# Two dense and three score banks of PSUM, woven attention work, and undivided differential maps in a two-layer encoder trunk

## The chip, the cores and the metric

The kernel runs on one core of a Trainium2 chip. The metric is the device time of one execution in microseconds (us). The kernel before takes 1228.05 us, the median of three runs (1227.83 to 1228.29). All engines of the core work side by side: PE multiplies matrices into the accumulators of PSUM, DVE and ACT do the elementwise work and alone read PSUM, POOL does elementwise work in SBUF, and SP issues the transfers.

## The reference

The input is 512 tokens of width 1024 in float32. There are two layers, and each has this shape:

```python
h = rmsnorm(x, attn_norm[l])
proj = einsum('bsd,de->bse', h, w_in[l])                 # 1024 -> 3072
sb_q, sb_k, sb_v, df_q, df_k, df_v = split(proj, ...)
# stick-breaking heads (8 of width 64), strictly causal:
#   w = sigmoid(z) * exp(reversed cumulative sum of log sigmoid(-z), without itself)
# differential heads (4, each with 2 maps of width 64), rope on q and k, causal by chunks of 64:
p = softmax(where(allowed, s, neg), axis=-1)
attn = p[:, :, 0] - lam * p[:, :, 1]
df_out = rmsnorm(attn @ v, subln_norm[l]) * (1 - lambda_init)
x = x + concat(sb_out, df_out) @ w_o[l]
h = rmsnorm(x, mlp_norm[l])
x = x + square(relu(h @ w_ff1[l])) @ w_ff2[l]            # 1024 -> 4096 -> 1024
```

A final rmsnorm follows. The rmsnorm over a differential head's output adds 1e-6 to the mean square before the root.

## The kernel before

Everything lies transposed: x is held as 8 tiles of 128 channels by 512 tokens. A product in float32 precision is made of three matmuls (function `three`, lines 260 to 262), with each operand split into a high and a low part: ACT rounds to the high part (L119 for weights, L207 for data) and DVE subtracts it (L120, L208). Weights come in units of 128x1024 through three raw buffers and two split buffers.

The attention of a layer is two streams woven into one. `dense()` makes the projections in blocks of 24 matmuls, one block for each 128 output channels, in the order d0 w0 d1 w1 ... s0 u0 ... s3 u3: d is the query and key of a differential pair, w its value, s the query and key of a stick-breaking pair, u its value. A block of the value is multiplied by the norm factor rbc (L400), then transposed through PSUM (L405, `vT`) and split (L412, L413). Differential queries and keys get rope from two DVE products (L463, L464) and two POOL sums (L471, L472); stick-breaking ones are scaled (L442). Their halves are moved by SP (L437), and for differential keys copied by ACT (L458), into stacked tiles. Behind the projections `dense()` makes the half of the output projection that takes the differential heads (`wo(1)`, 8 blocks of 12 matmuls, added to x at L699). The other half, `wo(0)`, comes when the attention is through.

`attn()` is the other stream. It goes through 24 units, 8 differential and 16 stick-breaking, and for unit i it makes the scores (`s1_df`, `s1_sb`), then the transposes of the weights of unit i-2 (`s2`, tiles T...), then the products with the values of unit i-3 (`s3`, tiles O...). In `s1_df` two matmuls (L499, L500) make a score tile; DVE masks it (L539 or L543) and reduces it to its negated maximum (L540 or L544), and ACT takes the exponential with the row sum (L552). Then both sums are inverted (L558), the second is multiplied by minus lambda (L559), POOL divides the first map (L560), and DVE adds the second (L561). In `s1_sb` ACT makes two sigmoids (L514, L515), DVE a product scan (L517), POOL the weight (L520).

A differential head's output is squared, and its norm factor goes through a transpose of the squares into PSUM and a reduction (`rms_a`, tile rs_d, L231 to L245), and through two matmuls that spread the factor (`rms_b`, tile rb_d, L253, L254). `start_norm` and `finish` issue the two in the next two steps of `attn()`.

The main loop takes one piece of `dense()` after the other and lets `attn()` run whenever its share of time, by costs written in the code, has come. This gives the order of the program; a scheduler of the framework then orders the instructions of each engine, and PE keeps that order. Each engine works through its queue strictly in order.

PSUM has eight banks of 128x512. They are shared out by tags: "t" has 2 (transposes T and vT, rs and rb tiles), "mm" has 3 (dense blocks, output projection, feed-forward), "s" has 2 (scores and two early projection blocks), and "o" has 1 (products with the values).

The feed-forward of a layer goes in two halves of 16 blocks (`block`, evicted at L783), each followed by 8 output blocks of 48 matmuls (L812). At the end of layer 1 the last units and the final norm are in `finale`.

Of the kernel before, what the change touches and what calls it, by code (L numbers as in the profile page):

```python
# [9 lines left out]
F32 = mybir.dt.float32  # L10
# [3 lines left out]
ALU = mybir.AluOpType  # L14
# [127 lines left out]
def trunk(ctx, tc, xT, w, gains, lamv, cos, sin, out):  # L142
# [6 lines left out]
    def bank(tag, name, bufs=2):  # L149
        return ps.tile([P, 512], F32, tag=tag, name=name, bufs=bufs)  # L150
# [76 lines left out]
    def rms_a(src, inv_n, col, name, eng, dgt):  # L227
        pt = bank("t", "rs_" + name)
        if RST and eng is not nc.gpsimd or RST == 2:
            for j in range(4):  # L230
                nc.tensor.transpose(pt[:, j * P : (j + 1) * P], src[:, j * P : (j + 1) * P], ident)  # L231
            nc.vector.tensor_reduce(out=ms, in_=pt.rearrange("p (j f) -> p j f", j=4), axis=AX.X, op=ALU.add)
            nc.vector.tensor_scalar(out=ms, in0=ms, scalar1=inv_n, scalar2=EPS, op0=ALU.mult, op1=ALU.add)
        else:
            for j in range(4):
                nc.tensor.matmul(pt[:, j : j + 1], src[:, j * P : (j + 1) * P], ones, start=True, stop=True)
            nc.vector.tensor_scalar(out=ms, in0=pt[:, 0:4], scalar1=inv_n, scalar2=EPS, op0=ALU.mult, op1=ALU.add)
        nc.gpsimd.tensor_tensor(out=col, in0=ms, in1=mhalf, op=ALU.pow)
        nc.vector.tensor_copy(chi, col)
        nc.vector.tensor_sub(clo, col, chi.bitcast(F32))  # L240
        dg_hi, dg_lo = dgt("dgh" + name), dgt("dgl" + name)
        idb = ident.unsqueeze(1).to_broadcast([P, 4, P])
        eng.tensor_mul(
            dg_hi.rearrange("p (j t) -> p j t", j=4), idb, chi.bitcast(F32).unsqueeze(2).to_broadcast([P, 4, P]))
        eng.tensor_mul(  # L245
            dg_lo.rearrange("p (j t) -> p j t", j=4), idb, clo.unsqueeze(2).to_broadcast([P, 4, P]))

        return dg_hi, dg_lo

    def rms_b(bc, name, dg):  # L250
        dg_hi, dg_lo = dg
        pb = bank("t", "rb_" + name)
        nc.tensor.matmul(pb, ones_r.to_broadcast([P, P]), dg_hi, start=True, stop=False)  # L253
        nc.tensor.matmul(pb, ones_r.to_broadcast([P, P]), dg_lo, start=False, stop=True)  # L254
        nc.scalar.copy(bc, pb)
# [14 lines left out]
    def block(name, tag="mm"):  # L270
        pt = bank(tag, name, 3 if tag == "mm" else 2)
# [23 lines left out]
    def finale(us, pool, small):  # L295
# [13 lines left out]
        def stage2(t, r):  # L309
            tk = slice(256 * t, 256 * t + 256)  # L310
            pb = bank("o", f"rb_f{t}", 1)
# [14 lines left out]
        tags = (("mm", 3), ("s", 2), ("mm", 3), ("s", 2), ("mm", 3))  # L326
        pts, sqs = [], []
        for t in range(2):
            tk = slice(256 * t, 256 * t + 256)
            for db in range(KC):  # L330
                tag, n = tags[(t * KC + db) % 5]
                sqf = pool.tile([P, 256], F32, tag="sqf", name=f"sqf{t}{db}", bufs=3)
                pt = bank(tag, f"fe{t}{db}", n)[:, 0:256]
# [17 lines left out]
    for l in range(L):  # L351
        with ExitStack() as actx:
# [45 lines left out]
            def evict_v(pt, kind, b, which):  # L398
# [3 lines left out]
                def rest():  # L402
                    tv = bank("t", f"vT{l}{kind}{b}")
# [16 lines left out]
            heads = {}  # L420

# [102 lines left out]
            def s1_df(u):  # L524
                b, half = u["b"], u["half"]
                st = {w: stacks[("d", b, w)] for w in "qk"}
                u["w"] = []
                for i in (2 * half, 2 * half + 1):
                    wd = P * (i + 1)
                    nm = f"{l}d{b}{i}"  # L530
                    sm = a3.tile([P, 6], F32, tag="sm", name="sm" + nm, bufs=4)
                    pr = []
                    both = bank("s", f"S{nm}") if wd <= 256 else None
                    for m in range(2):
# [13 lines left out]
                        if both is None or m == 1:  # L548
                            for mm, (pp, ss) in enumerate(pr):
                                if both is None and mm < m:  # L550
# [3 lines left out]
                                    accum_out=sm[:, 2 + mm : 3 + mm])  # L554
# [3 lines left out]
                    nc.vector.reciprocal(sm[:, 4:6], sm[:, 2:4])  # L558
                    nc.vector.tensor_mul(sm[:, 5:6], sm[:, 5:6], nlam[:, l : l + 1])  # L559
                    nc.gpsimd.tensor_mul(pr[0][:, 0:wd], pr[0][:, 0:wd], sm[:, 4:5].to_broadcast([P, wd]))  # L560
                    nc.vector.scalar_tensor_tensor(  # L561
                        out=pr[0][:, 0:wd], in0=pr[1][:, 0:wd], scalar=sm[:, 5:6], in1=pr[0][:, 0:wd],
# [34 lines left out]
            def s3(u):  # L597
                half, b, m, kind = u["half"], u["b"], u["m"], u["kind"]
                key = (kind, b, m)
                if half == 0:  # L600
                    heads[key] = bank("o", f"O{l}{kind}{b}{m}", 1)
# [61 lines left out]

            def attn():
                n = len(units)
                stage = 0
                for i in range(n + LAG3):
                    stage = stage + 1 if late else 0
                    if i < n:
# [3 lines left out]
                        yield from (s1_sb if u["kind"] == "s" else s1_df)(u)  # L673
                    if stage == 1:
                        yield start_norm()
                    if 0 <= i - LAG2 < n:
                        yield from s2(units[i - LAG2])
                    if stage == 2:
                        yield finish()
                        stage = 0  # L680
                    if 0 <= i - LAG3 < n:
                        while not ok(("v" + units[i - LAG3]["kind"], units[i - LAG3]["b"])):
                            yield 0
                        yield from s3(units[i - LAG3])
# [20 lines left out]
            def dense():  # L705
                step, held = 0, []
                if l == 0:
                    b = int(ORDER[0][1])
                    us = [W.next("x"), W.next("x")]
                    pts = [bank("mm", f"p0{i}", 3) for i in range(2)]  # L710
# [51 lines left out]
        with ExitStack() as fctx:  # L762
# [25 lines left out]
            for half in range(2):  # L788
                us = []
                for f in range(HC):  # L790
                    step = 0
                    for pt in block(f"f{l}_{half}_{f}"):
# [12 lines left out]
                for db in range(KC):  # L805
                    pt = bank("mm", f"f2_{l}{half}{db}", 3)
# [74 lines left out]
```

## Time and profile before

| what | us |
|---|---|
| median of three runs | 1228.05 |
| the profiled execution, its own time | 1228.06 |
| its span, first to last instruction | 1226.3 |
| attention of layer 0, about 0 to 262 | 262 |
| feed-forward of layer 0, about 262 to 611 | 349 |
| attention of layer 1, about 611 to 862 | 251 |
| feed-forward of layer 1 and finale, about 862 to 1226 | 364 |

The profile is of one execution. A row of a timeline has the start, the duration (of several instructions where they are merged), the engine, the line, the operation, the tile written and the tiles read, and in brackets how long the engine had been idle and what ended that. A row of waits has the waiting instruction, the one waited for, the sum, the number of times and the longest. PEld is PE's loading of weights, which runs beside the matmuls. PEclk is the share of full clock that PE was granted. Names in rows leave out buffer numbers: S0d is a differential score of layer 0, p0d its exponential map, T0d its transpose, O0d the product with the values; with s in place of d they are the stick-breaking ones. In the text a score's name goes on with the pair of heads, the row block and, for the two wide row blocks, the map: S0d121 is layer 0, pair 1, row block 2, map 1.

### The profile page before, as it was taken

What the parts mean: (1) busy time and instruction counts of PE and PEld (TensorE: products, weight loads), DVE (VectorE), ACT (ScalarE), POOL (GpSimd) and SP (SyncE); (2) the same over time, 40 slices, a digit from 0 to 9 for tenths busy, and PEclk for the clock granted to TensorE, in tenths of its full rate; (3) what the DMA queues carried; (4) which work ended last, traced back from release to release, by engine and by line L of the source; (5) the groups of instructions that cost most, each with busy time, mean ns of one, the idle gap of its engine ahead of it and who ended that gap; (6) DMA issues with size and microseconds to landing.
All of it is one profiled execution on the core that took longest, in us unless ns stands there. A gap on an engine that the chain in (4) does not pass through costs nothing.

```text
span 1226.3 us, 15312 instructions
## 1 busy us (share of the span) xinstructions
PE 1194.8 (97%) x5658; PEld 991.6 (81%) x5658; DVE 680.1 (55%) x1016; ACT 551.6 (45%) x932; POOL 202.3 (16%) x260
## 2 busy tenths in 40 slices
PE   9989999999999999999998999999999999999996
PEld 6777878888888888888887788888888888888886
DVE  7778877764532334433367887886544322544325
ACT  5666665553431234423347765665443221443114
POOL 1313543230000000001122344432100000000002
PEclk9999999999999999999999999999999999999998
DMA  7344443222233232232234344432223233232221
GB/s 250 78 137 133 119 136 104 68 87 104 87 102 101 88 103 95 94 104 90 100 97 132 110 128 118 123 103 70 94 96 103 89 101 103 86 103 91 90 95 69
DMA packets 46890, 128.16 MB, mean 105 GB/s; under 512 B 7264, under 2 KB 10336, under 8 KB 46816
## 3 DMA queue, kind: packets, MB, share of 16 engines
q1 hardware_dynamic: 46672, 127.17, 33.0%
q8 instruction: 45, 0.74, 0.2%
q14 instruction: 29, 0.24, 0.1%
q10 hardware_dynamic: 144, 0.02, 0.0%
HBM read 104.09 MB, written 2.10 MB: 87 GB/s over the span
## 4 chain that ended last, share of the span: by engine, by line
PE 85%; DVE 4%; ACT 3%; POOL 2%; issue 1%; SPq 1%; DMA 0%; DVEq 0%; POOLq 0%; ACTq 0%
PE f L260 19%; PE f L262 19%; PE f L261 19%; PE wo L261 2%; PE wo L260 2%; PE wo L262 2%; DVE wlo L120 1%; SPq L437 1%; PE T1s L580 1%; PE T0s L580 1%; PE O1s L609 0%; PE O0s L609 0%; PE O1s L608 0%; PE O0s L608 0%; PE S1d L499 0%
## 5 line engine op out<-in xcount | busy, mean ns | idle before, releaser
L119 ACT ACTIVATE whi<-raw 128x1024 fp32r<-128x1024 f32 (+2 forms) x198 | 203.2, 1028 | 480.0 <-PE f L261 427.2
L120 DVE TENSOR_TENSOR wlo<-raw,whi 128x1024 fp32r<-128x1024 f32 (+2 forms) x198 | 242.0, 1224 | 147.1 <-ACT whi L119 146.2
L260 PE MATMUL f<-h_hi,whi 128*128 128x512 f32 x512 | 199.4, 389 | 0.0
L262 PE MATMUL f<-h_hi,wlo 128*128 128x512 f32 x512 | 199.2, 389 | 0.0
L261 PE MATMUL f<-h_lo,whi 128*128 128x512 f32 x512 | 199.2, 389 | 0.0
L260 PE MATMUL f<-uh,whi 128*128 128x512 f32 x496 | 192.9, 389 | 0.0
L261 PE MATMUL f<-ul,whi 128*128 128x512 f32 x496 | 192.9, 389 | 0.0
L262 PE MATMUL f<-uh,wlo 128*128 128x512 f32 x496 | 192.9, 389 | 0.0
L783 DVE SCALAR_TENSOR_TENSOR ft<-f,rbc 128x512 f32<-128x512 f32 x64 | 44.3, 692 | 163.8 <-PE f L262 162.8
L262 PEld LDWEIGHTS f<-h_hi,wlo 128*128 128x128 f32 x512 | 96.1, 188 | 20.1
L261 PEld LDWEIGHTS f<-h_lo,whi 128*128 128x128 f32 x512 | 96.1, 188 | 20.0
L260 PEld LDWEIGHTS f<-h_hi,whi 128*128 128x128 f32 x512 | 96.1, 188 | 19.8
L261 PEld LDWEIGHTS f<-ul,whi 128*128 128x128 f32 x496 | 93.1, 188 | 19.4
L262 PEld LDWEIGHTS f<-uh,wlo 128*128 128x128 f32 x496 | 93.1, 188 | 19.4
L260 PEld LDWEIGHTS f<-uh,whi 128*128 128x128 f32 x496 | 93.1, 188 | 19.2
L221 POOL TENSOR_TENSOR ssq<-ssq,sq 128x512 f32<-128x512 f32 x21 | 34.8, 1656 | 374.3 <-ACT sq L220 365.2
L812 DVE TENSOR_TENSOR x<-x,f 128x512 f32<-128x512 f32 x32 | 22.0, 688 | 103.0 <-PE f L262 103.0
L342 POOL TENSOR_TENSOR ssq<-ssq,sqf 128x256 f32<-128x256 f32 x6 | 4.4, 737 | 338.4 <-ACT sqf L340 335.0
L208 DVE TENSOR_TENSOR ul<-fu,uh 128x512 fp32r<-128x512 f32 x64 | 44.1, 692 | 0.4 <-ACT uh L207 0.4
L207 ACT ACTIVATE uh<-fu 128x512 fp32r<-128x512 f32 x64 | 40.6, 635 | 2.0
L784 ACT ACTIVATE fu<-ft 128x512 f32<-128x512 f32 x64 | 39.7, 620 | 1.6 <-DVE ft L783 1.6
L520 POOL TENSOR_TENSOR sig1s<-sig1s,C1s 128x128 f32<-128x128 f32 (+3 forms) x32 | 30.0, 939 | 55.3 <-DVE C1s L517 40.9
(725 smaller groups left out, 2173.5 us busy)
## 6 DMA issues: line engine op xcount, KB each, us to landing
raw<-in_w SPq DMA_DIRECT2D x176, 512.0 KB, 3.5
raw<-in_w SPq DMA_DIRECT2D x16, 448.0 KB, 3.1
x<-in_xT SPq DMA_DIRECT2D x8, 256.0 KB, 4.4
out_xT<-y SPq DMA_DIRECT2D x8, 256.0 KB, 2.4
raw<-in_w SPq DMA_DIRECT2D x8, 128.0 KB, 4.3
cos_t<-in_cos SPq DMA_DIRECT2D x2, 256.0 KB, 3.8
sin_t<-in_sin SPq DMA_DIRECT2D x2, 256.0 KB, 3.6
kl0d0k<-l0d0k SPq DMA_DIRECT2D x8, 64.0 KB, 2.0
```

Source lines behind the costliest of these rows:

```text
L119: h = nc.scalar.activation(hi[:, a:b], raw[:, a:b], AF.Copy)
L120: self.last = h, nc.vector.tensor_tensor(out=lo[:, a:b], in0=raw[:, a:b], in1=hi[:, a:b].bitcast(F32), op=ALU.subtract)
L207: nc.scalar.activation(hi, src, AF.Copy)
L208: nc.vector.tensor_tensor(out=lo, in0=src, in1=hi.bitcast(F32), op=ALU.subtract)
L221: return s, eng.tensor_tensor(out=ssq, in0=ssq, in1=sq, op=ALU.add)
L260: nc.tensor.matmul(pt, ah, bh, start=first, stop=False)
L261: nc.tensor.matmul(pt, ah, bl, start=False, stop=False)
L262: nc.tensor.matmul(pt, al, bh, start=False, stop=last)
L520: nc.gpsimd.tensor_mul(sig[:, 0:wd], sig[:, 0:wd], C[:, 1 : wd + 1])
L580: nc.tensor.transpose(pt[:, off : off + P], u["w"][qi][:, kb * P : (kb + 1) * P], ident)
L783: nc.vector.scalar_tensor_tensor(out=t, in0=pt, scalar=0.0, in1=rbc, op0=ALU.max, op1=ALU.mult)
L784: nc.scalar.activation(uu, t, AF.Square)
```

## The change

It has four parts.

1. PSUM: "mm" gets 2 banks, "s" 3. A new tag "any" takes the five of both in the turn mm, s, s, mm, s; it is used by the feed-forward, the finale and `wo(0)`. `vT` of the stick-breaking values and `rb_d` go from "t" to "s". In layer 0 the projection block at step 16 goes to "s" too, and in layer 1 that at 16 instead of that at 32.
2. `attn()`: the rest of a step (start of the norm, transposes of unit i-2, end of the norm, values of unit i-3) is a generator of its own, and one piece of it is issued behind every piece of the scores, where before it came behind all scores of the unit.
3. The maps are not divided: the first map stays as the exponential gave it, and the second is added with the factor minus lambda times the first sum over the second. POOL's division L560 is gone.
4. The head's output is so larger by the first row sum, which its rmsnorm takes out again. Only the 1e-6 has to grow by the square of that sum: `start_norm` makes a small tile `floor` from the kept sums (`tops`), and `rms_a` adds it.

```diff
-    def bank(tag, name, bufs=2):
-        return ps.tile([P, 512], F32, tag=tag, name=name, bufs=bufs)
+    banks = {"t": 2, "mm": 2, "s": 3, "o": 1}
+    turn = [0]
+
+    def bank(tag, name):
+        if tag == "any":
+            tag = ("mm", "s", "s", "mm", "s")[turn[0] % 5]
+            turn[0] += 1
+        return ps.tile([P, 512], F32, tag=tag, name=name, bufs=banks[tag])
...
-    def rms_a(src, inv_n, col, name, eng, dgt):
+    def rms_a(src, inv_n, col, name, eng, dgt, floor=None):
...
-            nc.vector.tensor_scalar(out=ms, in0=ms, scalar1=inv_n, scalar2=EPS, op0=ALU.mult, op1=ALU.add)
+            if floor is None:
+                nc.vector.tensor_scalar(out=ms, in0=ms, scalar1=inv_n, scalar2=EPS, op0=ALU.mult, op1=ALU.add)
+            else:
+                nc.vector.scalar_tensor_tensor(
+                    out=ms, in0=ms, scalar=inv_n, in1=floor, op0=ALU.mult, op1=ALU.add)
...
-    def rms_b(bc, name, dg):
+    def rms_b(bc, name, dg, tag="t"):
         dg_hi, dg_lo = dg
-        pb = bank("t", "rb_" + name)
+        pb = bank(tag, "rb_" + name)
...
-        tags = (("mm", 3), ("s", 2), ("mm", 3), ("s", 2), ("mm", 3))
...
-                pt = bank(tag, f"fe{t}{db}", n)[:, 0:256]
+                pt = bank("any", f"fe{t}{db}")[:, 0:256]
...
-                    tv = bank("t", f"vT{l}{kind}{b}")
+                    tv = bank("s" if kind == "u" else "t", f"vT{l}{kind}{b}")
...
+                if half == 0:
+                    tops[b] = a3.tile([P, 4], F32, tag="top", name=f"top{l}{b}", bufs=3)
+                top = tops[b]
...
-                    sm = a3.tile([P, 6], F32, tag="sm", name="sm" + nm, bufs=4)
+                    sm = a3.tile([P, 5], F32, tag="sm", name="sm" + nm, bufs=4)
+                    sums = (top[:, i : i + 1], sm[:, 2:3])
...
-                    nc.vector.reciprocal(sm[:, 4:6], sm[:, 2:4])
-                    nc.vector.tensor_mul(sm[:, 5:6], sm[:, 5:6], nlam[:, l : l + 1])
-                    nc.gpsimd.tensor_mul(pr[0][:, 0:wd], pr[0][:, 0:wd], sm[:, 4:5].to_broadcast([P, wd]))
+                    nc.vector.reciprocal(sm[:, 3:4], sums[1])
                     nc.vector.scalar_tensor_tensor(
-                        out=pr[0][:, 0:wd], in0=pr[1][:, 0:wd], scalar=sm[:, 5:6], in1=pr[0][:, 0:wd],
+                        out=sm[:, 4:5], in0=sums[0], scalar=nlam[:, l : l + 1], in1=sm[:, 3:4],
+                        op0=ALU.mult, op1=ALU.mult)
+                    nc.vector.scalar_tensor_tensor(
+                        out=pr[0][:, 0:wd], in0=pr[1][:, 0:wd], scalar=sm[:, 4:5], in1=pr[0][:, 0:wd],
                         op0=ALU.mult, op1=ALU.add)
...
             def start_norm():
                 b, os_, sqo, rc = late[0]
-                dgs[b] = rms_a(sqo, 1.0 / P, rc, f"d{l}{b}", nc.gpsimd, tr)
+                floor = a3.tile([P, 4], F32, tag="floor", name=f"floor{l}{b}")
+                nc.vector.scalar_tensor_tensor(
+                    out=floor, in0=tops[b], scalar=EPS, in1=tops[b], op0=ALU.mult, op1=ALU.mult)
+                dgs[b] = rms_a(sqo, 1.0 / P, rc, f"d{l}{b}", nc.gpsimd, tr, floor)
...
-                rms_b(rb, f"d{l}{b}", dgs[b])
+                rms_b(rb, f"d{l}{b}", dgs[b], "s")
...
+            def behind_scores(i, stage):
+                n = len(units)
+                if stage == 1:
+                    yield start_norm()
+                if 0 <= i - LAG2 < n:
+                    yield from s2(units[i - LAG2])
+                if stage == 2:
+                    yield finish()
+                if 0 <= i - LAG3 < n:
+                    while not ok(("v" + units[i - LAG3]["kind"], units[i - LAG3]["b"])):
+                        yield 0
+                    yield from s3(units[i - LAG3])
 
             def attn():
...
+                    rest = behind_scores(i, stage)
...
-                        yield from (s1_sb if u["kind"] == "s" else s1_df)(u)
...
+                        front = (s1_sb if u["kind"] == "s" else s1_df)(u)
+                        for cost in front:
+                            yield cost
+                            nxt = 0
+                            while nxt == 0:
+                                nxt = next(rest, None)
+                                if nxt is not None:
+                                    yield nxt
+                    yield from rest
...
-                        pt = bank("mm", f"wo{l}{half}{db}", 3)
+                        pt = bank("mm" if half else "any", f"wo{l}{half}{db}")
...
-                        for pt in block(name, "s" if step in (24, 32) else "mm"):
+                        for pt in block(name, "s" if step in ((16, 24, 32), (16, 24))[l] else "mm"):
...
-                    for pt in block(f"f{l}_{half}_{f}"):
+                    for pt in block(f"f{l}_{half}_{f}", "any"):
...
-                    pt = bank("mm", f"f2_{l}{half}{db}", 3)
+                    pt = bank("any", f"f2_{l}{half}{db}")
```

More of the change, by code (lines that the diff above doesn't have):

```diff
@@ L270, in block @@
     def block(name, tag="mm"):
-        pt = bank(tag, name, 3 if tag == "mm" else 2)
+        pt = bank(tag, name)
         u = W.next("px" if name[0] == "p" else "1")
@@ L310, in stage2 @@
             tk = slice(256 * t, 256 * t + 256)
-            pb = bank("o", f"rb_f{t}", 1)
+            pb = bank("o", f"rb_f{t}")
             for j in range(2):
@@ L600, in s3 @@
                 if half == 0:
-                    heads[key] = bank("o", f"O{l}{kind}{b}{m}", 1)
+                    heads[key] = bank("o", f"O{l}{kind}{b}{m}")
                 o = heads[key][:, half * 256 : half * 256 + 256]
@@ L709, in dense @@
                     us = [W.next("x"), W.next("x")]
-                    pts = [bank("mm", f"p0{i}", 3) for i in range(2)]
+                    pts = [bank("mm", f"p0{i}") for i in range(2)]
                     for c, i in [(c, i) for c in range(5) for i in range(2)] + [(c, i) for i in range(2) for c in (5, 6, 7)]:
```

13 lines of the change are left out of this document (2 added, 11 removed).

## The prediction

> **What bounds the kernel now.** I read the page's busy shares, then windows by stage, then what PE waited for, then the timeline around the longest waits.
>
> ```profile
> span 1226.3 us, 15312 instructions
> PE 1194.8 (97%) x5658; PEld 991.6 (81%) x5658; DVE 680.1 (55%) x1016; ACT 551.6 (45%) x932; POOL 202.3 (16%) x260
> ...
> PE 85%; DVE 4%; ACT 3%; POOL 2%; issue 1%; SPq 1%; DMA 0%; DVEq 0%; POOLq 0%; ACTq 0%
> ```
>
> PE bounds it: 97% busy, 85% of the chain that ended last. The change keeps PE's 5646 matmuls and their sizes (the built programs have the same count), so only idle time and lost clock can go. Where they lie, by windows (columns: length, then PE, PEld, DVE, ACT, POOL busy, then PEclk, DMA share, GB/s):
>
> ```profile
> 262.00:611.00 349.00, 349.00 (x1543) 289.02 (x1543) 140.16 (x158) 114.76 (x145) 14.52 (x9) 1.00 0.29 97
> 862.00:1208.00 346.00, 346.00 (x1558) 287.58 (x1557) 139.54 (x165) 110.79 (x145) 5.70 (x6) 1.00 0.28 92
> 70.50:74.50 4.00, 3.52 (x15) 3.48 (x16) 3.31 (x10) 3.98 (x12) 1.09 (x2) 0.62 0.39 98
> 98.30:102.50 4.20, 3.89 (x15) 3.30 (x16) 3.61 (x9) 3.69 (x9) 1.50 (x2) 0.59 0.72 219
> 651.00:655.00 4.00, 3.21 (x9) 2.83 (x10) 2.18 (x10) 3.90 (x12) 1.01 (x2) 0.59 0.41 103
> ```
>
> Both feed-forward stages, 695 us of the span, have no idle PE and a granted clock of 1.00: 349/1543 = 0.226 us a matmul. Three short stretches of the attention have a low clock; they lost 0.38 x 4.0 = 1.5, 0.41 x 4.2 = 1.7 and 0.41 x 4.0 = 1.6 us, 4.8 together. PE's own waits:
>
> ```profile
> PE S1d L499 <- ACT p1d L552: 6.4, 4, 3.0
> PE S0d L499 <- ACT p0d L552: 6.3, 5, 2.2
> ...
> PE rb_d L253 <- DVE zl L208: 2.0, 2, 1.0
> ...
> PE T1s L580 <- DVE vs L413: 1.6, 1, 1.6
> PE T0s L580 <- DVE vs L413: 1.6, 1, 1.6
> ```
>
> 12.7 us are differential scores (L499) waiting until exponentials (L552) have read one of two score banks; rb_d and T0s/T1s (5.2) wait for one of two "t" banks. What is left are waits of the start and of the finale, which the change leaves as they are. Two of the score waits of layer 0 and their cause:
>
> ```profile
> 58.44 0.67 DVE L464 TENSOR_TENSOR v0d2k<-p0d2k,sin_t 128x512 f32<-128x512 f32 x1
> ...
> 60.40 1.28 POOL L471 TENSOR_TENSOR u0d2q<-u0d2q,v0d2k 128x512 f32<-128x512 f32 x1
> ...
> 60.48 1.61 DVE L561 SCALAR_TENSOR_TENSOR p0d<-p0d,sm0d,p0d 128x384 f32<-128x384 f32 x1 [0.21 <-POOL p0d L560]
> ...
> 62.10 0.11 DVE L539 MEMSET S0d<- 64x64 f32 x1
> ...
> 62.25 0.67 ACT L552 ACTIVATE p0d<-S0d,sm0d 128x512 f32<-128x512 f32 x1
> ...
> 62.59 0.67 DVE L540 TENSOR_REDUCE sm0d<-S0d 128x1 f32<-128x512 f32 x1
> 62.82 0.19 ACT L552 ACTIVATION_READ_ACCUMULATOR p0d<-S0d,sm0d 128x1 f32 x1
> ...
> 63.06 0.39 PE L499 MATMUL S0d<-st0d1k,st0d1q 128*128 128x256 f32 x1 [1.67 <-ACT p0d L552]
> ...
> 65.39 1.04 POOL L560 TENSOR_TENSOR p0d<-p0d,sm0d 128x512 f32<-128x512 f32 x1 [3.71 <-DVE sm0d L558]
> ...
> 68.84 1.26 ACT L458 ACTIVATE st0d2k<-h0d2k 32x512 fp32r<-32x512 f32 x2
> ...
> 70.12 0.37 ACT L552 ACTIVATE p0d<-S0d,sm0d 128x128 f32<-128x128 f32 x1
> ...
> 70.98 0.44 PE L499 MATMUL S0d<-st0d1k,st0d1q 128*128 128x384 f32 x1 [2.01 <-ACT p0d L552]
> ...
> 71.72 2.01 ACT L119 ACTIVATE whi<-raw 128x1024 fp32r<-128x1024 f32 x2
> ...
> 88.28 0.40 PE L260 MATMUL p0w3v<-h_hi,whi 128*128 128x512 f32 x1
> ...
> 94.03 1.50 DVE L561 SCALAR_TENSOR_TENSOR p0d<-p0d,sm0d,p0d 128x256 f32<-128x256 f32 x1
> ...
> 98.61 0.70 PE L499 MATMUL S0d<-st0d2k,st0d2q 128*128 128x512 f32 x1 [2.16 <-ACT p0d L552]
> ...
> 99.85 0.62 DVE L561 SCALAR_TENSOR_TENSOR p0d<-p0d,sm0d,p0d 128x384 f32<-128x384 f32 x1
> ```
>
> L561 took 1.61 us while POOL ran L471, 0.62 at 99.85 without it; DVE's memset, the exponential and PE stand behind it. At 70.98 the exponential stood behind key copies (L458) on ACT. Two waits of layer 1, the first its longest:
>
> ```profile
> 646.43 3.19 ACT L458 ACTIVATE st1d1k<-h1d1k 32x512 fp32r<-32x512 f32 x5
> ...
> 649.63 1.28 ACT L552 ACT_TABLE_LOAD   x1
> ...
> 651.79 0.69 PE L499 MATMUL S1d<-st1d0k,st1d0q 128*128 128x384 f32 x1 [2.99 <-ACT p1d L552]
> ...
> 697.59 0.50 PE L499 MATMUL S1d<-st1d2k,st1d2q 128*128 128x512 f32 x1 [2.07 <-ACT p1d L552]
> ```
>
> **The change part by part**, against the profiled execution: 1228.06 us, span 1226.3 and 1.8 around it; the median of the three runs is 1228.05, so nothing is shifted.
>
> *Feed-forward, second half of the output projection: five banks in turn for three.* PE never waited there, so no gain; more banks in the same order hold nothing up: 0. If that cover went, a wait would stand on x L812, which DVE does in 0.69 us (row below) against a block of 24 x 0.226 = 5.4.
>
> ```profile
> L812 DVE TENSOR_TENSOR x<-x,f 128x512 f32<-128x512 f32 x32 | 22.0, 688 | 103.0 <-PE f L262 103.0
> L560 POOL TENSOR_TENSOR p0d<-p0d,sm0d x16: 401/759/2096, 54.9 to 127.4; 128x128 f32<-128x128 f32 x4, 128x256 f32<-128x256 f32 x4, 128x384 f32<-128x384 f32 x4, 128x512 f32<-128x512 f32 x4
> L559 DVE TENSOR_TENSOR sm1d<-sm1d,nlam x16: 141/160/1004, 652.0 to 728.7; 128x1 f32<-128x1 f32 x16
> ```
>
> The first is a group of the page (mean in ns behind the comma), the others are rows by line (minimum, median, maximum in ns).
>
> *Undivided maps.* 32 POOL multiplications L560 go, 0.4 to 2.1 us each. On DVE L558, L559 and L561 stay three instructions (L559 becomes a three-operand one), and eight small "floor" instructions come, 8 x 0.16 = 1.3 us by L559's median; DVE is 55% busy, cost 0. The chain from exponential to transpose loses its POOL step (1.04 at 65.39), and DVE no longer stops for it. L471/L472 stay, so L561 can still be caught.
>
> *Third score bank, scores woven.* In the built order of the changed kernel each differential score asks for the bank of the score three before, and I compared how much PE work lies between with how long the bank was held here.
> Layer 0, wait at 63.06: the banks asked for are those of scores that ended 3.3 to 5 us before. A bank needs memset 0.11, reduction 0.68, exponential 0.67 and 0.19 of reading back, 1.6 in a row and some 2 to 3 us among its neighbours without the blocked L561. The 1.67 goes.
> Late next there is the transpose T0d0010 of block 0: it now comes 5.6 us after its last score, whose map needs up to 3 us for the same steps, a reciprocal, two rope products (0.67 each, L464) that now stand ahead of it on DVE, and L561 behind L471 again (1.28 and then its own 0.62), some 7.2 with 0.3 of small steps: a new wait of 1.6. Then S0d121 asks for the first bank of block 1, whose exponentials stand behind three splits and four copies (0.63 each) on ACT: 1.3; the next score 0.2; then p0d3q, whose weight split (1.05, in L119 at 71.72) stands behind four exponentials: 1.0; one more score 0.3. New waits 4.4 in place of 4.3 (1.67, 0.44 before T0d, 2.01 and small ones): this block gains nothing. Ends: 0 if ACT drains its copies in the holes, 6 if the queue slips by one more split.
> Wait at 98.61: the score now asks for a bank freed 6 us earlier: 2.16 goes, and 1.7 of clock with it. But T0d1011 needs the "t" bank of rs_d00, whose reduction stands on DVE behind the blocked L561 of 94.03: ready 95.53 + 0.67 = 96.2, which is 7.9 us after p0w3v began at 88.28. In the changed order T0d1011 comes 6.7 us after that: 1.2 new.
> Layer 1: the 2.99 at 651.79 stays: the copies, the table load and the exponentials keep their order on ACT, and S1d021 comes where S1d020 came, within 0.1 us; its 1.6 of clock stays too. The other three waits of the row (6.4 - 3.0 = 3.4) go: the banks asked for there are free 0.2 us or more before.
>
> *vT of the stick-breaking values and rb_d in score banks.* This takes them off the "t" banks: 2.0 + 1.6 + 1.6 = 5.2 go. The score banks have room: every stick-breaking score comes at least 0.4 us after its bank is read. Two transposes per layer come 0.2 us early for their bank: -0.4.
>
> *Two dense banks for three.* A block's bank is asked for one block later, 5.4 us plus the woven attention. In the row below the worst of the later blocks, p0w3v, was read 8.6 us after its last matmul:
>
> ```profile
> 96.05 0.40 PE L262 MATMUL p0w3v<-h_hi,wlo 128*128 128x512 f32 x1
> 104.19 0.68 DVE L400 TENSOR_TENSOR tv0w<-p0w3v,rbc 128x512 f32<-128x512 f32 x1
> DVE x L699 <- PE wo L262: 4.6, 8, 0.8
> ```
>
> There the changed order leaves 6.9 us, but on DVE tv0w3 now comes right behind the reduction of the last score, about 3.3 us after: 0. If it stayed at 8.6 it would cost 1.7, and -1.7 to 0 are the ends. With two output-projection blocks in turn DVE still waits for PE (L699). Blocks held back until rbc exists (the first four) get score banks that no score needs yet: 0.
>
> *The clock.* Its three drops followed 2.01, 2.16 and 2.99 us without work; 2.07 us before 697.59 and 1.67 before 63.06 drew none as deep. One drop goes (1.7), one stays (layer 1), and the one at 70.5 stays: PE will idle 2.8 us in four pieces within 4 us there.
> The Trainium skill ("TensorE: Matmul & The Clock Gate", "What's actually happening") lets the clock fall only after an idle window of about 3.4 us. The drops after 2.01 and 2.16 us disagree. By the page the pieces near 70 us would cost no clock and the sum would be 1.5 us lower.
>
> *Sum.* Gains: layer 0 score waits 6.3 and T0d 0.4, layer 1 3.4, "t" banks 5.2, clock 1.7: 17.0. New: 4.4 + 1.2 + 0.4 = 6.0. Net 11.0; small refills behind each wait that goes (0.1 to 0.2 us, some eight of them) add about 1. 1228.0 - 12.0 = **1216.0 us**, 1.0% faster. Ends: no new waits and both clock drops of layer 0 gone, 12 + 6 + 1.5 = 19.5 less: 1208.5. Layer 0's score part (6.7 + 1.7 = 8.4) given back whole: only 3.4 + 5.2 remain, less 2 for slips of one small instruction: 1221.5.
>
> **The rivals.**
> *A: the waits only move.* ACT and DVE, not banks, hold the scores (for it: L458 ahead of the exponentials at 68.84 and 646.43). PE asks sooner and waits for the same queues; the "t" banks alone are gained: 1228 - 5.2 = 1222.8, down to 1221. Against it: 98.61 and the later waits of layer 1 are cured by distance alone.
> *B: two dense banks starve, slower.* 64 blocks take turns on two banks, 24 projections and 8 of the output projection in each layer. If DVE reads a block more than one block late, PE stops at each. It decides against the change once the mean lateness passes by 12/64 = 0.19 us; at 0.3 us each: 64 x 0.3 - 12 = 7 slower, 1235. For it: 8.6 at p0w3v. Against it: the reads at the end of the attention, where DVE waits for PE.
> *C: five banks in turn let the clock oscillate in the feed-forward.* Where one-block-ahead filling let PE pause between groups, the clock would drop as it did at 70.5; 1% of 695 us at 0.6 is 2.8 lost, and 5% turns the sum to 1230. Against it: three banks in turn already run at 1.00 with no pause.
> The Trainium skill ("TensorE: Matmul & The Clock Gate", "A second HAM failure mode: psum-queue depth-cycling") describes such a loss from cycling through PSUM banks; the two windows do not bear it out.
> *D: nothing to measure.* Gains and new waits cancel within 0.2%, about what a measurement of this kernel can tell from no change: 1228.
>
> **How the numbers follow.** Forecast (1208 to 1221) 0.72; A 0.14; B 0.09; C 0.01; D 0.04. Faster is the forecast and A: 0.86; same 0.04; slower 0.10. Leaving B to D and the edge of A outside, the range is 1207 to 1224.
>
> **What would show it.** PE's waits for L552's successor down from 12.7 us to between 6 and 8, most of it near 65 to 73 us and at the 651.79 of before; no wait of rb_d, T0s or T1s above 0.5; a clock near 1.00 where 98.3 to 102.5 was; POOL below 185 us; feed-forward windows with no idle PE. Wrong would be: waits of dense blocks (first matmul of a p or wo block) behind DVE reads, or layer 1's first wait gone as well.

## The result and the profile after

The changed kernel takes 1216.89 us, the median of four runs (1216.56 to 1218.76), against 1228.17 of the kernel before on the same chip (1227.83 to 1228.69): a ratio of 0.9918, with a 95% interval of 0.9906 to 0.993 (the two medians by themselves give 0.9908). The profiled execution took 1217.13 us with a span of 1215.3, so 11.0 us of span are gone. The page's first lines after the change:

```profile
span 1215.3 us, 15244 instructions
PE 1190.8 (98%) x5658; PEld 990.5 (81%) x5658; DVE 678.8 (56%) x1024; ACT 549.2 (45%) x932; POOL 171.2 (14%) x228
```

PE has 5658 records in both traces. POOL lost 31 us of work, DVE kept its own. The windows of the two feed-forward stages and of three short stretches (columns as in the prediction; PEclk is the third number from the right):

```profile
254.00:603.00 349.00, 349.00 (x1543) 289.06 (x1543) 140.11 (x158) 114.53 (x145) 14.71 (x9) 1.00 0.29 97
852.00:1197.00 345.00, 344.33 (x1549) 286.07 (x1549) 141.06 (x166) 110.53 (x146) 5.57 (x6) 1.00 0.28 92
69.20:73.20 4.00, 3.71 (x9) 2.38 (x10) 3.01 (x12) 3.98 (x11) 0.00 (x0) 0.62 0.40 101
98.30:102.50 4.20, 3.08 (x16) 2.38 (x15) 3.41 (x8) 4.13 (x9) 0.00 (x0) 1.00 0.42 105
644.00:648.00 4.00, 4.00 (x12) 3.37 (x13) 2.32 (x10) 3.53 (x10) 0.00 (x0) 0.62 0.41 101
```

The feed-forward is as it was, but for 0.67 us of idle PE in the second. Of the three clock drops before, that of 98.3 is gone and two remain. These windows of 4.0 us catch 0.38 x 4.0 = 1.5 us of each; a whole drop is 3.41 us at half clock, so 1.7 us (last section). PE's waits after the change:

```profile
PE S1d L508 <- ACT p1d L565: 3.1, 1, 3.1
PE S0d L508 <- ACT p0d L565: 2.2, 2, 1.9
...
PE vT1w L413 <- DVE tv1w L408: 1.7, 1, 1.7
PE vT0w L413 <- DVE tv0w L408: 1.7, 2, 1.1
...
PE S1d L508 <- DMA st1d3q<-l1d3k: 1.0, 1, 1.0
...
PE rb_d L263 <- issue: 0.7, 2, 0.4
PE T0d L594 <- DVE S0d L552: 0.7, 1, 0.7
PE rs_m L237 <- POOL ssq L227: 0.7, 1, 0.7
```

The scores waited 12.7 us for exponentials and now wait 5.3, a little less than the 6 to 8 that the prediction named as its sign. T0s and T1s no longer appear, and rb_d has 0.7 left. New are vT0w (1.1 of its 1.7; 0.6 was there before), vT1w, a score that waits for a transfer, and rs_m at the start of the second feed-forward.

Where the gain arises, by the start of the last matmul of a block in the two traces (up to 2 us of attention work can lie on the other side of a block, so the ends of stages are the firm numbers):

| last matmul of | before | after | gained so far |
|---|---|---|---|
| p0w2v | 66.2 | 64.3 | 1.9 |
| p0s0q | 107.5 | 102.5 | 5.0 |
| attention of layer 0 (second half of wo) | 261.8 | 254.0 | 7.8 |
| p1d2q | 658.5 | 650.6 | 7.9 |
| p1w3v | 699.2 | 689.8 | 9.4 |
| p1s1q | 732.7 | 724.8 | 7.9 |
| attention of layer 1 | 861.8 | 850.0 | 11.8 |
| end | 1219.5 | 1208.6 | 10.9 |

Layer 0 gave 7.8 us, layer 1 4.0, and 0.9 came back behind it, 0.7 of it in the wait of rs_m.

### The profile page after: what moved, and what is told of

Its sections match the earlier page's. It is cut to its first block, busy times and chain, and to the rows that moved or that the text cites. A ratio compares the mean times of both kernels' runs of the same rounds, so it can differ in the third digit from the quotient of the medians.

```text
span 1215.3 us, 15244 instructions
## 1 busy us (share of the span) xinstructions
PE 1190.8 (98%) x5658; PEld 990.5 (81%) x5658; DVE 678.8 (56%) x1024; ACT 549.2 (45%) x932; POOL 171.2 (14%) x228
## 5 line engine op out<-in xcount | busy, mean ns | idle before, releaser
L529 POOL TENSOR_TENSOR sig0s<-sig0s,C0s 128x128 f32<-128x128 f32 (+3 forms) x32 | 25.9, 809 | 58.1 <-DVE C0s L526 41.8
```

The source lines that it names most:

```text
L529: nc.gpsimd.tensor_mul(sig[:, 0:wd], sig[:, 0:wd], C[:, 1 : wd + 1])
```

## The experiments

Each ratio is against the kernel before, run on the same chip in turn; that of the whole change is 0.9918.

**Parts alone.** *banks* is part 1 of the change alone, *weave* part 2 alone, *maps* parts 3 and 4 alone; *noweave* is the changed kernel with the old `attn()`, so without part 2.

```diff
 # banks: before, with
+    banks = {"t": 2, "mm": 2, "s": 3, "o": 1}
...
 # maps: before, with
-                    nc.gpsimd.tensor_mul(pr[0][:, 0:wd], pr[0][:, 0:wd], sm[:, 4:5].to_broadcast([P, wd]))
...
 # weave: before, with
+                        for cost in front:
+                            yield cost
...
 # noweave: after, with
-                        front = (s1_sb if u["kind"] == "s" else s1_df)(u)
+                        yield from (s1_sb if u["kind"] == "s" else s1_df)(u)
...
```

> The kernel before with the first part of the change alone: the new sharing of PSUM, with vT of the stick-breaking values and rb_d in score banks and five banks in turn in the feed-forward; scores not woven, maps divided. Theory of the prediction: the waits of rb_d, T0s and T1s (5.2 us) go, two small ones come (0.4); a third score bank without weaving cures only the scores that ask for the bank of the unit before, about half of the 12.7 us, and about 4 us of new waits behind DVE and ACT stay: about 1220 us (1217 to 1223). Rival A, waits only move: the t banks alone are gained, 1223. Rival B, two dense banks starve: 1235.

Measured: 0.9981 (0.997 to 0.9991), 1225.9 us: 2.3 us gained by the ratio where 8 were expected. PE's waits in its trace show where the rest went:

```profile
PE vT1w L409 <- DVE tv1w L404: 2.7, 1, 2.7
PE p0d3q L266 <- ACT whi L119: 2.5, 1, 2.5
...
PE T0s L584 <- POOL sig0s L524: 1.1, 1, 1.1
```

The scores' own rows fell from 12.7 to 6.0 us, as much as the theory said. But PE then came to a weight split that stood behind key copies and splits of transposes on ACT (2.5), to vT1w (2.7), and T0s and T1s, freed of the bank, waited 1.1 each for POOL's weights. The waits moved, as rival A says, and so far that even its 1223 us was not reached.

> The kernel before with the undivided maps alone: POOL's division and the DVE work it stands ahead of leave the chain from exponential to transpose; banks and order as before. Theory of the prediction: the banks, not the chain behind the exponential, hold PE; only T0d's 0.44 us and a part of the blocked DVE go: 1226 to 1228 us. Rival: POOL beside DVE is what makes the score waits, and the division is half of POOL's part in them: 1222 us or less.

Measured: 0.9985 (0.9976 to 0.9994), 1225.7 us, 0.3 below the theory's 1226 to 1228 and far from the 1222 of the rival, which falls.

> The kernel before with the woven scores alone: two score banks, maps divided. Theory of the prediction: other blocks' transposes and values between two scores give each bank one piece more of time (0.4 to 0.8 us for each piece), so score waits of about 0.5 us go and those of 1.7 to 3 us shrink by that much, some of it given back where a transpose now comes earlier than its map: 1224 us (1221 to 1227). Rival A, the queues of ACT and DVE hold the scores whenever they come: 1228 us.

Measured: 0.9988 (0.9979 to 0.9997), 1226.5 us: 1.5 us, in the theory's range and near its poor end. Its trace has the score rows down to 7.1 us (and 0.5 of a stick-breaking score), and in their place waits that were not there: T0d for a transfer 1.4, rs_d 1.1, a further T0d 1.0.

> The changed kernel without weaving: banks and undivided maps as changed, scores of a unit in a row as before. Theory of the prediction: weaving and the third bank are needed together for the scores, so this stands between: 1219 us (1217 to 1222), with waits of the fourth score of a unit for the bank of its first. Rival: the bank alone does it, and this is as fast as the changed kernel, 1217 us.

Measured: 0.9956 (0.9944 to 0.9969), 1222.1 us. The rival falls: banks and maps without weaving are 4.7 us short of the whole change. The theory is right that this stands between, but its 1219 is missed by 3. The largest single place, in the timeline of its DVE and PE, is worth 3.2 of the 5.8 us of span (1.5 of wait, 1.7 of clock):

```profile
91.96 1.50 DVE L575 SCALAR_TENSOR_TENSOR p0d<-p0d,sm0d,p0d 128x256 f32<-128x256 f32 x1
...
98.31 0.61 DVE L575 SCALAR_TENSOR_TENSOR p0d<-p0d,sm0d,p0d 128x384 f32<-128x384 f32 x1
98.84 0.68 DVE L238 TENSOR_REDUCE ms<-rs_d 128x4 f32<-128x512 f32 x1
...
99.58 0.55 PE L594 MATMUL T0d<-edge,p0d 128*128 128x128 f32 x3 [2.23 <-DVE ms L238]
```

With the unit's scores in a row, their reductions and map sums fill DVE, the reduction of rs_d stands behind them, and the transpose waits 2.2 us for its "t" bank; the clock then was 0.57 from 101 to 105. In the changed kernel the same wait is 0.73 us. The score rows are 8.3 us against its 5.3, and T0s and T1s wait 1.1 each for POOL.

The three parts alone gain 0.19, 0.15 and 0.12%, 0.46 together; the first two together gain 0.44; all three gain 0.82. Banks and maps add within the intervals (0.34 apart, 0.44 together); with weaving the whole is nearly twice the sum of the parts. The rows of banks show why: one obstacle is cleared, and PE then stands at the next.

**The whole change less one piece.** *nomaps* has POOL's division back (parts 3 and 4 undone); *tvt* has vT and rb_d back in "t"; *ffmm* has two banks in place of five in turn; *mm3s2* has three dense and two score banks.

```diff
 # nomaps: after, with
+                    nc.gpsimd.tensor_mul(pr[0][:, 0:wd], pr[0][:, 0:wd], sm[:, 4:5].to_broadcast([P, wd]))
...
 # tvt: after, with
-                    tv = bank("s" if kind == "u" else "t", f"vT{l}{kind}{b}")
+                    tv = bank("t", f"vT{l}{kind}{b}")
...
 # ffmm: after, with
-            tag = ("mm", "s", "s", "mm", "s")[turn[0] % 5]
+            tag = "mm"
 # mm3s2: after, with
-    banks = {"t": 2, "mm": 2, "s": 3, "o": 1}
+    banks = {"t": 2, "mm": 3, "s": 2, "o": 1}
-            tag = ("mm", "s", "s", "mm", "s")[turn[0] % 5]
+            tag = ("mm", "s", "mm", "s", "mm")[turn[0] % 5]
```

> The changed kernel with the maps divided again, as before: POOL's 32 divisions stand again between exponential and transpose; banks and weaving as changed. Theory of the prediction: POOL and DVE have room, the division is worth next to nothing: 1217 to 1219 us. Rival: with the transposes woven in early, the chain behind the exponential decides, and the division (0.4 to 2.1 us each) costs PE new waits at T0d and T1d: 1221 us or more.

Measured: 0.9957 (0.9944 to 0.997), 1222.0 us. The rival's time holds: within the whole change the undivided maps are worth 0.39%, some 4.8 us, where the prediction had them at nothing. In layer 0 the division made the waits that the rival named (timeline of DVE, POOL and PE):

```profile
62.99 1.04 POOL L564 TENSOR_TENSOR p0d<-p0d,sm0d 128x512 f32<-128x512 f32 x1
64.07 0.75 DVE L565 SCALAR_TENSOR_TENSOR p0d<-p0d,sm0d,p0d 128x512 f32<-128x512 f32 x1 [1.02 <-POOL p0d L564]
64.87 0.33 PE L584 MATMUL T0d<-edge,p0d 128*128 128x128 f32 x1 [0.89 <-DVE p0d L565]
664.72 1.50 DVE L565 SCALAR_TENSOR_TENSOR p1d<-p1d,sm1d,p1d 128x256 f32<-128x256 f32 x1 [0.51 <-POOL p1d L564]
673.45 0.33 PE L409 MATMUL vT1w<-edge,tv1w 128*128 128x128 f32 x1 [2.66 <-DVE tv1w L404]
```

Two such waits of T0d cost 1.6 us there, but the score wait near 69 gave way to one of 1.1 us for a weight split, with no clock drop behind it, and this execution left the attention of layer 0 at the same time as the changed kernel (254.2 against 254.0). The loss is in layer 1, not at the T1d that the rival names: DVE stands still for 0.5 us for POOL's division at 664.72 and needs 1.16 us for a split at 670.43 that takes 0.69 in the changed kernel; the product tv1w so comes 1.1 us later (672.72 against 671.61), vT1w waits 2.66 instead of 1.75, and the clock, which stayed at 1.00 after 1.75, fell to 0.57 from 674 to 678 (1.7 us). The rest is smaller waits behind it. So a DVE that stops for POOL delays the value's product, not only the transposes.

> The changed kernel with vT of the stick-breaking values and rb_d back in the two t banks. Theory of the prediction: the waits of rb_d, T0s and T1s come back, 5.2 us less 0.4: 1222 us. Rival: weaving alone has already taken most of them (the kernel with weaving alone shows 3.2 us for the same rows): 1219 us or less.

Measured: 0.9954 (0.9939 to 0.9969), 1222.8 us: 4.4 us lost, nearer to the theory's 4.8 than to the rival's 2. Its rows:

```profile
PE rb_d L263 <- DVE vdl L421: 2.1, 1, 2.1
...
PE T0s L594 <- DVE fl0s L214: 0.7, 1, 0.7
```

The rival is right on T0s and T1s, 0.7 each where 1.6 stood before. What makes up the sum is rb_d in layer 1, which now waits until vT1w is read from its "t" bank (vdl); the clock behind it was 0.57 from 706.3 to 710.3 (1.7 us).

> The changed kernel with the feed-forward, the first half of the output projection and the finale on the two dense banks alone, in place of five in turn. Theory of the prediction: a block's bank is read within 1 us and asked for again after 5.4 us, so the number of banks is worth nothing there: 1217 us, feed-forward without idle PE. Rival: two banks leave PE idle at the turn of blocks, 0.1 us or more for each of some 130 blocks: 1230 us or more.

Measured: 0.9919 (0.9906 to 0.9932), 1217.7 us, the changed kernel's ratio. Five banks in turn are worth nothing in the feed-forward, as predicted, and with two PE is never idle in it:

```profile
252.00:601.00 349.00, 349.00 (x1543) 289.21 (x1542) 141.95 (x162) 116.03 (x148) 16.65 (x10) 1.00 0.31 97
```

Two banks do show at the seams: at 851.04, 1190.37 and 1192.67 a first matmul waits 0.4 us for DVE to read its bank, 1.2 in all, while the wait of rs_f in the finale is 1.3 shorter than in the changed kernel.

> The changed kernel with three dense and two score banks, as before the change; weaving, undivided maps, and vT and rb_d in the score banks stay. Theory of the prediction: the third score bank is what weaving needs; score waits come back by half, and vT and rb_d now wait for score banks too: 1222 us (1219 to 1226). Rival: two dense banks cost what the third score bank brings (waits of vT0w and vT1w, which stand behind late reads): 1217 us or less.

Measured: 0.9987 (0.9977 to 0.9997), 1226.2 us: nearly all of the gain is lost, 0.2 us more than the theory's range has. But the trace does not let all of it go to the score banks. Score rows come to 7.5 us (4.3 + 2.3 + 0.9) for 5.3; against that stand two waits of dense blocks that neither kernel has, with a slow clock behind them:

```profile
PE p0d2k L270 <- ACT whi L119: 1.9, 1, 1.9
PE p0d2q L272 <- DVE wlo L120: 1.4, 1, 1.4
```

In this kernel the projections of layer 0 came in another order, and PE reached two weight halves before they were split, at 44.8 and 46.9; from 46.31 to 53.14 the clock was 0.50, 3.4 us lost. That is 6.7 of the 10.4 us of span; some 3.7 are left for the score banks. The kernel before has the same three and two banks and no such waits, so the numbers of banks alone do not make them. The run refutes its rival (vT1w fell from 1.7 to 0.5, and that did not pay), but it does not size the third bank cleanly.

**The waits that stayed or came.** *late_vt* issues the transposes of the differential values 2 us later; *table* loads the exponential's table early in layer 1; *copies* does that and moves eight key copies in each layer from ACT to SP's transfers; *both* is copies and late_vt together.

```diff
 # late_vt, both
-                defer(DLY_V, rest)
+                defer(DLY_V if kind == "u" else 5.5, rest)
 # copies, both
-                                defer(KC_GAP * (4 * j + 2 * m + i + 1), copy_k(k[d_, m, :], hi[rk, :]))
+                                if (l, b) in ((0, 2), (1, 1)):
+                                    move(k[d_, m, :], hi[rk, :])
+                                else:
+                                    defer(KC_GAP * (4 * j + 2 * m + i + 1), copy_k(k[d_, m, :], hi[rk, :]))
 # table, copies, both
+                            if l == 1 and step == 4:
+                                pre = a3.tile([P, 1], F32, tag="pre", name="pre")
+                                nc.scalar.activation(pre, ones, AF.Exp)
```

> The changed kernel with the transposes of the differential values (vT0w, vT1w) issued 2 us of work later. Theory: they wait because DVE multiplies the block (tv0w, tv1w) behind the reduction of the last score and the sum of two maps, 1 to 2 us later than PE comes; 2 us of dense work ahead of them cover that: the rows of vT0w and vT1w (3.4 us) go: 1213.5 us (1213 to 1215). Rival: the products with these values then start late, and the wait moves to O0d or to the next transposes: 1217 us.

Measured: 0.9916 (0.9901 to 0.993), 1218.1 us. The theory's time falls and the rival's is nearer, though the waits went to other places than the rival names. The vT0w and vT1w rows are gone, and in their place PE waits for a weight split and for transfers:

```profile
PE p0d3q L270 <- ACT whi L119: 2.1, 1, 2.1
...
PE S0d L508 <- DMA st0d3q<-l0d3k: 1.7, 1, 1.7
PE S1d L508 <- DMA st1d3q<-l1d3k: 1.5, 1, 1.5
```

The clock has a part in it. Two of the six executions, with a mean granted clock of 0.995 and 0.997, took 1215.3 and 1215.5 us, and the other four, at 0.992 and 0.993, 1217.5 to 1219.7. The profiled one is of the slower ones: behind layer 1's first score its clock was 0.50 for 6.83 us, 3.4 us lost where the changed kernel lost 1.7.

> The changed kernel with the eight key copies that stand on ACT ahead of the first exponentials (of d2 in layer 0, d1 in layer 1) made by transfers of SP, and the table of the exponential loaded by a small exponential of ones early in layer 1 (its result is not used). Theory of the prediction: ACT's queue, not the banks, makes the two waits that stayed (2.1 us near 69 with 1.4 us of clock, 3.3 us near 644 with 1.2 to 1.6 of clock). Layer 1: 1.9 us of copies and 1.28 of table load go from ahead of the exponentials, so the wait and its clock loss go, 4.5 us; layer 0: the exponentials then stand on DVE's reduction that ends at 67.5, 0.85 us earlier, so 1 to 2 us: 1211 us (1209 to 1213). Rival: eight more transfers at 0.6 us each on SP's queue hold back stacked halves or weights by 4.8 us, and PE waits for these: 1217 us or more.

Measured: 0.9865 (0.985 to 0.988), 1211.1 us, 5.8 us below the changed kernel by the medians and the value that the theory gave. Waits and clock of its trace:

```profile
PE p1d3q L270 <- ACT whi L119: 1.7, 1, 1.7
...
PE S1d L511 <- ACT p1d L568: 0.9, 1, 0.9
...
PE S0d L511 <- ACT p0d L568: 0.9, 3, 0.4
68.50:72.50 4.00, 3.35 (x15) 2.65 (x15) 3.99 (x15) 3.26 (x9) 0.00 (x0) 1.00 0.43 107
636.00:640.00 4.00, 3.53 (x16) 2.95 (x17) 3.55 (x15) 3.40 (x12) 0.00 (x0) 1.00 0.43 107
```

The two waits went from 3.1 and 2.2 us to 0.9 each, and the clock stayed at 1.00 at both places; the two drops that are gone are 3.4 of the 7.8 us of span. The wait of vT1w gave way to one for a weight split (p1d3q, 1.7), that of vT0w in front of 100 is gone. The transfers cost nothing that shows: the score's wait for a transfer is 0.9 where it was 1.0. The split by layers was otherwise than expected: this execution (1209.3, the fastest of its four) gained 3.7 us in layer 0, where 1 to 2 were expected, and 3.3 in the attention of layer 1, where 4.5 were.

> The changed kernel with both edits of the two runs beside it: later transposes of the differential values, and key copies and table load out of the way of the first exponentials. Theory: different places, so the gains add: 1207.5 us (1206 to 1211). Rival: they meet the same queues, and the sum of both is not above the larger: 1211 us or more.

Measured: 0.9854 (0.984 to 0.9868), 1209.7 us. The gains do not add as the theory said; the interval overlaps that of copies, so whether the later transposes bring anything is open. It is the fastest kernel of the study, 1.5% below the one before.

> The changed kernel with the early load of the exponential's table alone (a small exponential of ones early in layer 1, its result not used); all key copies stay on ACT. Theory: the load's 1.28 us go from ahead of the first exponentials of layer 1, so the wait at 644 shrinks from 3.3 to 2.0 us; the clock fell after 2.1 us near 69, so the drop there stays or is smaller: 1215.6 us (1214 to 1216), and the key copies are then the larger part of the 5.8 us that both edits brought. Rival: the table load lay beside the reduction that the exponentials need anyway, and nothing comes of it: 1217 us.

Measured: 0.9912 (0.9895 to 0.9929), 1216.5 us, which is no difference from the changed kernel. The theory of the load falls, and the reason is not the rival's. ACT and PE around the place, and below them ACT in the changed kernel:

```profile
638.84 3.18 ACT L467 ACTIVATE st1d1k<-h1d1k 32x512 fp32r<-32x512 f32 x5
642.03 0.37 ACT L565 ACTIVATE p1d<-S1d,sm1d 128x128 f32<-128x128 f32 x1
...
642.89 0.44 PE L508 MATMUL S1d<-st1d0k,st1d0q 128*128 128x384 f32 x1 [3.18 <-ACT p1d L565]
...
638.63 3.18 ACT L467 ACTIVATE st1d1k<-h1d1k 32x512 fp32r<-32x512 f32 x5
641.82 1.28 ACT L565 ACT_TABLE_LOAD   x1
643.11 0.37 ACT L565 ACTIVATE p1d<-S1d,sm1d 128x128 f32<-128x128 f32 x1
```

The load did go from ahead of the exponentials: the same five copies (3.18 us) stand there in both, and the first exponential begins 1.1 us earlier. But PE's order changed with it. The changed kernel has eight matmuls of p1d2q ahead of the waiting score, this one two; the other six (6 x 0.226 = 1.4 us) stand behind it. So PE came to the score 1.15 us earlier too (639.71 against 640.86) and waited 3.2 as before. What the load alone would bring with PE's order kept, no run shows. So the gain of copies is that of the copies, or of the copies and the load together; it is not the load alone.

## Why the prediction was right, point by point

The time came within 1 us of the forecast, by the mechanism it named: distance to the score banks, "t" banks cleared, one clock drop gone. The two layers, however, missed in opposite directions. By the prediction's steps layer 0 gains 6.3 + 0.4 + 2.6 + 1.7 less 4.4 + 1.2 + 0.2 = 5.2, layer 1 3.4 + 2.6 less 0.2 = 5.8, to which its refills add about 0.5 each; measured were 7.8 and 4.0 - 0.9 = 3.1. That the two misses nearly cancel, and the sum so comes within 1 us, is luck. Step by step, with the rows of the changed kernel's timeline on which it turns:

```profile
65.76 2.56 ACT L467 ACTIVATE st0d2k<-h0d2k 32x512 fp32r<-32x512 f32 x4
66.57 1.00 DVE L557 TENSOR_REDUCE sm0d<-S0d 128x2 f32<-128x256 f32 x2
68.33 0.37 ACT L565 ACTIVATE p0d<-S0d,sm0d 128x128 f32<-128x128 f32 x1
69.19 0.44 PE L508 MATMUL S0d<-st0d1k,st0d1q 128*128 128x384 f32 x1 [1.95 <-ACT p0d L565]
...
91.04 1.51 DVE L575 SCALAR_TENSOR_TENSOR p0d<-p0d,sm0d,p0d 128x256 f32<-128x256 f32 x1
92.47 0.68 DVE L238 TENSOR_REDUCE ms<-rs_d 128x4 f32<-128x512 f32 x1
93.29 0.30 PE L594 MATMUL T0d<-edge,p0d 128*128 128x128 f32 x1 [0.73 <-DVE S0d L552]
...
98.36 0.69 DVE L553 TENSOR_REDUCE sm0d<-S0d 128x1 f32<-128x512 f32 x1
98.96 0.68 DVE L408 TENSOR_TENSOR tv0w<-p0w3v,rbc 128x512 f32<-128x512 f32 x1
99.79 0.63 PE L413 MATMUL vT0w<-edge,tv0w 128*128 128x128 f32 x4 [1.12 <-DVE tv0w L408]
```

- *Feed-forward in five banks: 0.* Right: 349 us at clock 1.00, and the same with two.
- *Undivided maps: 0.* Wrong as a part of the whole. On the kernel before they were worth 1.9 us by their own run, but inside the change 4.8 (nomaps). The step looked for a price in instructions and in DVE's share of busy time; the price was in order, since DVE stops for POOL with the products of values queued behind. The sum did not miss it because its lateness figures for the changed kernel already had no POOL step in them.
- *Layer 0 near 65 to 73: 4.4 new for 4.3 gone.* The place is right and so is the cause: four copies on ACT stand ahead of the exponentials, which begin 0.8 us after both reductions have ended (67.57). The size is not. The waits of T0d0010 (1.6) and of the weights of p0d3q (1.0) did not come, S0d121 took 1.95 for 1.3 and the next 0.29: 2.2 in all. The clock drop stayed, as said.
- *Wait at 98.61 gone with 1.7 of clock, T0d1011 new.* Right in both, the second smaller than said: 1.00 in that window, and T0d waits 0.73 at 93.29 for 1.2, behind the reduction of rs_d, which stood behind an L575 of 1.51 us.
- *Layer 1's first wait stays.* Right: 3.1 us and 1.7 of clock. The run with the copies and the table load moved shows that ACT's queue holds it, not the banks.
- *The other three score waits of layer 1 (3.4).* Gone, but the step missed what is late next. A score waits 0.96 for a transfer of its own stacked half, and vT1w 1.75 for DVE.
- *"t" banks: 5.2 less 0.4.* Right: rb_d 0.7, no T0s or T1s; the run that puts them back loses 4.4.
- *Two dense banks: 0; tv0w3 3.3 us after p0w3v.* This is the step that failed. No dense block waited for its bank, so the 0 held, but tv0w3 ended at 99.64, 5.1 us after the last matmul of p0w3v (begun at 94.1 and 0.39 long), behind the last reduction and a map sum. Its own transposes, not the next block, wait for it, 1.12 us, and in layer 1 those of w2 wait 1.75 in the same way; the prediction looked only at the bank. (The 8.6 us that it has for p0w3v before are 8.4 by its two rows.)
- *rs_m, 0.67 at the start of the second feed-forward,* was not foreseen either. It waits for POOL's last sum of squares, which ended at 855.76. It is no fixed price of the change: late_vt, copies and table keep all four parts and have no such wait. What sets it stays open.
- *The clock.* The three drops before were 1.7 us each, 5.1 together; the prediction's 4.8 comes from windows that cut two of them. The drop behind 1.95 us of idle near 69 is again one that the Trainium skill ("TensorE: Matmul & The Clock Gate", "What's actually happening") would not give by its idle window of about 3.4 us. In the 3.41 us ahead of that drop PE was busy for 1.18. The same section says that the window is free-running; with that the traces agree: within each, the changes of clock lie whole multiples of 3.413 us apart (below).

Rival A was partly true: banks alone and late_vt show a wait moving to the next queue. Rival B, C and D fell.

## What to carry to other kernels

When one engine bounds the time and stalls on several others in turn, price the parts of a change together: a wait removed is worth only the distance to the next thing that is late, and the three parts here gave 0.46% apart and 0.82% together. For each wait that goes, write down every later instruction of the bounding engine whose input stands in the same queues, the transposes of a result as well as the reuse of its buffer. And where a wait is put down to a buffer, look at what stands ahead of the releasing instruction on its own engine: moving eight small copies in each layer off ACT, together with the early load of a table, brought half as much again as the whole change.

## What the runs showed of the hardware

The clock does not fall by the length of an idle time alone. Idle PE of 3.1 us at layer 1's first score was followed by a clock of 0.62 in the changed kernel, and in ffmm by none, for the same wait; 2.66 us of vT1w in nomaps drew 0.57, and 1.75 of the same wait in the changed kernel nothing. What decides shows when the time is cut into steps. From the first rise to the end of the work a drop is, in all traces, a clock of 0.50 for 3.41 us, in two cases (mm3s2, late_vt) for 6.83, and within a trace the changes of clock lie whole multiples of 3.413 us apart: the two drops of the changed kernel begin at 70.19 and 643.62, 168 such steps. The step ahead of a drop and the drop, in the changed kernel, and then the two steps over which the same wait is spread in ffmm:

```profile
640.21:643.62 3.41, 0.65 (x3) 0.19 (x1) 1.42 (x3) 3.37 (x7) 0.00 (x0) 1.00 0.38 96
643.62:647.04 3.42, 3.07 (x8) 2.61 (x9) 1.57 (x7) 3.40 (x12) 0.00 (x0) 0.50 0.47 116
...
640.61:644.02 3.41, 1.49 (x7) 0.91 (x5) 2.26 (x6) 3.37 (x5) 0.00 (x0) 1.00 0.42 106
644.02:647.43 3.41, 2.22 (x10) 1.87 (x11) 1.94 (x9) 3.40 (x12) 0.00 (x0) 1.00 0.39 99
```

PE was busy for 0.65 of 3.41 us in the first case, for 1.49 and 2.22 in the second: the same wait lies in one step there and across two here. Over all steps at full clock between 24 and 1200 us in the 14 traces (the kernel before, the changed one and the 12 experiments), the 23 in which PE was busy for less than 0.43 of the step all had a drop behind them, of the ten from 0.44 to 0.53 three had, and of the 4731 above that none. This is read off the traces; no run was made to vary it by itself.

A drop is worth 1.7 us here (half of 3.41), so executions of one kernel differ without any difference in the work: those of the changed kernel with a mean granted clock of 0.995 took 1216.6 and 1216.7 us, the one with 0.992 took 1218.8. A gain that removes a wait of 2 to 3 us is to be counted with a part of a drop.
